# Moving the S5 tables, their loads and their parameters: which engine, which queue, which step

## The chip, the core and the metric

The kernel runs on one core of a Trainium2 chip (TensorE, VectorE, ScalarE, GpSimd and SyncE, with 16 DMA engines). The metric is the time of one execution in microseconds (us) on the device; less is better. In the profile the engines are PE, DVE, ACT, POOL and SP; TensorE's weight loads are PEld.

## What is computed

One layer of a hybrid encoder on 2048 tokens of 1024 channels, in float32. Cut to what matters here:

```python
h = rms_norm(x, norm_gain)
proj = einsum('bsd,de->bse', h, w_in)
q, k, v, z_attn, u_ssm, z_ssm, g = split(proj, SPLITS)          # 512,128,128,512,512,512,2048
attn = windowed_gqa(q, k, v, attn_sink, rel_bias_table) * silu(z_attn)
y = gelu(s5_bidirectional(u_ssm, a_re, a_im, log_dt, b_re, b_im, c_re, c_im, ssm_d))
y = y * sigmoid(y @ w_glu + b_glu)
ssm = y * silu(z_ssm)
merged = sigmoid(g_attn) * (attn @ w_branch_attn) + sigmoid(g_ssm) * (ssm @ w_branch_ssm)
return rms_norm(x + merged @ w_out, final_norm_gain)

def s5_bidirectional(u, ...):        # 32 groups of 16 channels, 64 states per group and direction
    for d in range(2):
        dt = exp(log_dt[d]);  a_bar = exp(lam * dt);  b_bar = b * (a_bar - 1) / lam
        x[t] = a_bar * x[t-1] + b_bar @ u[t]      # d = 1 runs backwards
        y   += Re(c @ x)
    y += d_skip * u
```

## The kernel before, in words

Every matrix product is made with each operand split into a high and a low part, by three matmuls (`mm3`, L215 to L225: L219 high by high, L220 low of h, L221 low of w). A projection is one 128-column strip of `w_in` against one block of 512 tokens: 8 x 3 = 24 matmuls.

**Stage one** (to some 170 us) makes h for four blocks of 512 tokens (`make_h`, its transposes on TensorE at L274), projects u, k and v of each (strips u0 to u3, k, v in the list `wlist`, index i), stores u in channel order as uS, and stores the h of blocks 0 and 1 in DRAM as hS (`spill`). v is turned over by transposes at L388. The parameters of the SSM are loaded and computed in it as well (`ssm_params`, L432 to L659): DMA issues on SP first (L443 for a, L455 for c), then eleven transposes (L468, L476), then 288 small VectorE instructions (most of them L481) that make powers and products of the states' factors.

**Stage two** (to some 1140 us) projects q, z_attn, z_ssm and the gates, and beside it runs a chain of side work: the SSM, then attention. **Stage three** is the GLU, the branches, the output projection and the last norm.

What sets the order: the program is written out in one pass, and side work is a Python generator. `mm3` calls `turn` or `tick` four times in a projection; each gives every side generator credit of half its rate, and a generator goes on to its next `yield` for each unit of credit. So a "step" (the work between two yields) of the chain falls behind a fixed number of projection matmuls, and every engine takes its instructions in the order in which they were written. Weights are split a strip ahead: the high part on ScalarE (L162), the low part on GpSimd in four pieces (`low_part`, L154). Loads are issued on SP (`nc.sync`), stores on ScalarE (`A`).

The SSM (`ssm`) works in 8 frames of 4 groups. Tokens are cut into 256 pieces of 8 (M = 256, T = 8). A frame i has 18 steps:

- `inject` (four times): W times U on TensorE (L829), copied into X by ScalarE (L830, L831);
- for each half: `rotate` by the tables ec, es (L838, L839, L841 on VectorE), `scan` (L850), rotate back, `high_h` (L857 on ScalarE) and `low_h` (L862 on VectorE), which make the parts Hh, Hl of the states;
- `emit` for each half: M times U (L872) and ws times H on TensorE, copied to Y by ScalarE (L880).

Beside it the frame prepares what later frames need. `prep_w`, `prep_o` and `prep_e` are tables of products (helper `product`, L684 to L686: two products and their sum or difference, tiles wt, wo, ec and es), all three on GpSimd but for frame 0. `mats` transposes wt on TensorE (L767) into Wh, Wl (L770, L761). `zmat` flips the sign of wo on ScalarE (`sign_o`, L731, and ncc, L733), multiplies it by b on TensorE (L792, L799) into Z, and stores Z to DRAM as zS (L803); `load_m` reads it back as the band matrix Ml in four DMAs (L809), and `load_u` reads the next U in four (L744), all on SP. `split_o`, `split_m`, `split_u` make high and low parts (L719 on ScalarE, L720 on VectorE); `mirror_e` fills the other half of ec, es (L716 on ScalarE).

```python
            if i == 0:
                yield from zmat(0)
                load_m(0)
...
                prep_o(nx)
...
            if nx:
                load_m(nx)
            if nn:
                load_u(nn, 0)
                load_u(nn, 1)
```

Of the kernel before, what the change touches and what calls it, by code (L numbers as in the profile page):

```python
# [21 lines left out]
NBLK = 4  # L22
COL_Q, COL_K, COL_V, COL_ZA, COL_U, COL_ZS, COL_G = 0, 512, 640, 768, 1280, 1792, 2304
G, P, C, T = 32, 64, 16, 8
M = S // T
GB = 4
RATE1 = 1.336
RATE2 = 1.237
RATE3 = 1.499
# [7 lines left out]
def kernel(  # L37
# [9 lines left out]
    nc = tc.nc  # L47
# [3 lines left out]
    out = out[0]  # L51
# [379 lines left out]
    eye = prm.tile([128, C], F32, name="eye")  # L431

    def ssm_params(pool):
        n_ = [0]
# [11 lines left out]
        for d in range(2):  # L446
            V.tensor_copy(raw[:, 2, d * 64:(d + 1) * 64], dt2[:, d:d + 1].to_broadcast([32, 64]))
        for src, dst in ((ssm_b_re, bb_re), (ssm_b_im, bb_im)):
# [20 lines left out]
        re, im, ld = sm(), sm(), sm()  # L469
        V.tensor_copy(re, pt[:, 0:32])  # L470
        V.tensor_copy(im, pt[:, 32:64])
        V.tensor_copy(ld, pt[:, 64:96])
        for i, dst in enumerate((cc_re, cc_im)):
# [4 lines left out]
        yield 1.5  # L478

        def tt(o, a, b, op):  # L480
            V.tensor_tensor(o, a, b, op)  # L481
            return o
# [44 lines left out]
        xi = tt(sm(), im, dt_, ALU.mult)  # L527
        yield 4
        sc, e1 = exp_parts(xr)
        ex = stt(sm(), e1, 1.0, sc, ALU.add, ALU.mult)  # L530
        em1 = tt(sm(), e1, sc, ALU.mult)
        stt(em1, sc, -1.0, em1, ALU.add, ALU.add)
        yield 4
        k = rnd(xi, 0.3183098861837907)
# [18 lines left out]
        cs = ts(sm(), cm, 1.0, None, ALU.add, None)  # L553
        yield 5
        ar = tt(pw_re[:, :, 1], ex, cs, ALU.mult)
# [33 lines left out]
        for i in range(2, T + 1):  # L589
            cmul(pw_re[:, :, i], pw_im[:, :, i], pw(i // 2), pw(i - i // 2))  # L590
        yield 8
        f, b_ = slice(0, 64), slice(64, 128)
        for dst_i, dst_o, src in ((wi_re, wo_re, pw_re), (wi_im, wo_im, pw_im)):
# [3 lines left out]
            V.tensor_copy(dst_o[b_], src[b_, :, T:0:-1])  # L597
        yield 8
        tb = [pool.tile([128, G, C], F32, tag=f"tb{i}", name=f"tb{i}") for i in range(4)]
# [7 lines left out]
        tt(bb_im, tb[2], tb[3], ALU.add)  # L607
        yield 4
        e8 = ts(sm(), xr, 8.0, None, ALU.mult, None)
# [42 lines left out]
        powers(el_re, el_im, 16)  # L652
        yield 4
        cmul(*hi(1), lo(8), lo(8))
        powers(eh_re, eh_im, 8)
        unit(el_re, el_im, 16)
        unit(eh_re, eh_im, 8)
        yield 4


    def ssm(pool):
# [10 lines left out]
        def product(o, p, q, eng):  # L672

            for n, (a, b, c, d, op) in enumerate(
                ((p[0], q[0], p[1], q[1], ALU.subtract), (p[0], q[1], p[1], q[0], ALU.add))
            ):
                for g in range(0, o[n].shape[1], 2):
                    gs = slice(g, g + 2)
                    if eng is Q:
                        tmp = [pool.tile([128, 2, T, C], F32, tag=f"t{m}", name=f"t{m}") for m in range(2)]  # L680
                    else:
                        r = rtile().rearrange("p g r m -> p (g r m)")
                        tmp = [r[:, m * 256:m * 256 + 256].rearrange("p (g j c) -> p g j c", g=2, c=C) for m in range(2)]
                    eng.tensor_tensor(tmp[0], a[:, gs], b[:, gs], ALU.mult)  # L684
                    eng.tensor_tensor(tmp[1], c[:, gs], d[:, gs], ALU.mult)  # L685
                    eng.tensor_tensor(o[n][:, gs], tmp[0], tmp[1], op)  # L686
# [53 lines left out]
        def load_u(i, half):  # L740
            lo = pool.tile([128, 2, M], F32R, tag=f"U{half}l", name=f"U{half}l", bufs=2)
            raw = lo.bitcast(F32)
            for j in range(2):
                nc.sync.dma_start(out=raw[:, j], in_=chan(uS, i * GB + half * 2 + j))  # L744
            raw_u[i, half] = lo, raw
# [29 lines left out]
        def zmat(i):  # L775

            g0 = i * GB
            s = st[i]
            sign_o(i)
            yield  # L780
            wo = raw_o[i]
            Z = pool.tile([128, 15 * C], F32, tag="Z", name="Z")
            pf, pb = bank("s2"), bank("s2")

            def two(t, g):

                return t[:, g0 + g:g0 + g + 2].rearrange("p g c -> p (g c)")

            for d, pt, o0, c0 in ((f, pf, 16, 0), (b_, pb, 0, 16)):
                for n, bt in enumerate((bx_re, bx_im)):  # L790
                    for g in range(GB):
                        PE.matmul(  # L792
                            pt[g * 32:(g + 1) * 32, o0:o0 + 112], two(bt, g)[d],
                            wo[n][:, g].rearrange("p j c -> p (j c)")[d, c0:c0 + 112], start=n == 0, stop=n == 1,
                        )
                yield
            for n, (bt, ct) in enumerate(((bx_re, cc_re[:, g0:g0 + GB]), (bx_im, s["ncc"]))):
                for g in range(GB):
                    PE.matmul(pf[g * 32:(g + 1) * 32, 0:16], two(bt, g), ct[:, g], start=n == 0, stop=n == 1)  # L799
            V.tensor_copy(Z[:, 0:112], pb[:, 0:112])  # L800
            V.tensor_copy(Z[:, 112:240], pf[:, 0:128])
            V.scalar_tensor_tensor(Z[:, 112:128], eye, dd[:, i:i + 1], Z[:, 112:128], ALU.mult, ALU.add)
            nc.sync.dma_start(out=zS[i], in_=Z)  # L803

        def load_m(i):
            lo = pool.tile([128, GB, 128], F32R, tag="Ml", name="Ml")
            raw = lo.bitcast(F32)
            for g in range(GB):
                nc.sync.dma_start(  # L809
                    out=raw[:, g],  # L810
                    in_=bass.AP(
                        tensor=zS.tensor, offset=zS.offset + (i * 128 + g * 32) * 15 * C,
                        ap=[[C, T], [15 * C, C], [1, 128]],
                    ),
                )
            st[i]["m"] = (lo, raw)
# [66 lines left out]

        def frame(i):

            nx = i + 1 if i + 1 < NB else None
            nn = i + 2 if i + 2 < NB else None
            ms = mats(nx) if nx else None
            zs = zmat(nx) if nx else None
            inject(i, 0)  # L890
            yield
            inject(i, 1)
            yield
            rotate(i, 0, 0)
            inject(i, 2)
            yield
            scan(i, 0)
            inject(i, 3)
            yield
            if i == 0:  # L900
                yield from zmat(0)
                load_m(0)
            rotate(i, 0, 1)
            if nx:
                next(ms)
                prep_e(nx, 0)
            yield
            split_o(i)
            if nx:
                next(ms)  # L910
                prep_o(nx)
            yield
            high_h(i, 0)
            rotate(i, 1, 0)
            if nx:
                next(ms, None)
            if nn:
                prep_w(nn)
            yield
            low_h(i)  # L920
            scan(i, 1)
            yield
            split_m(i)
            rotate(i, 1, 1)
            if nx:
                prep_e(nx, 1)
            yield
            yield
            yield from emit(i, 0)
            yield  # L930
            high_h(i, 1)
            if nx:
                mirror_e(nx, 0)
                next(zs)
            yield
            low_h(i)
            if nx:
                split_u(nx, 0)
                next(zs)
            yield  # L940
            if nx:
                split_u(nx, 1)
                mirror_e(nx, 1)
                next(zs)
            yield
            yield from emit(i, 1)
            if nx:
                next(zs, None)
            yield
            if nx:  # L950
                load_m(nx)
            if nn:
                load_u(nn, 0)
                load_u(nn, 1)
            st.pop(i)
            yield

        raw_o, ph = {}, {}
        load_u(0, 0)
        load_u(0, 1)  # L960
        prep_w(0, V)
        prep_e(0, 0)
        prep_e(0, 1)
        prep_o(0, V)
        for _ in range(3):
            yield
        split_u(0, 0)
        split_u(0, 1)
        yield from mats(0)
        mirror_e(0, 0)  # L970
        mirror_e(0, 1)
        load_u(1, 0)
        load_u(1, 1)
        prep_w(1)
        for i in range(NB):
            yield from frame(i)

# [238 lines left out]
    with tc.manual_schedule():  # L1216
# [85 lines left out]
        for b in range(NBLK):  # L1302
            gen = None
            for i, key in enumerate(wlist):
# [4 lines left out]
                if i == 1 and b + 1 < NBLK:  # L1309
                    gen = add_side(make_h(xp, b + 1), RATE1)  # L1310
                    if b + 2 < NBLK:
                        load_x(xp, b + 2)
                if b == 2 and i == 3:
                    s2.close()
                    spool = s1.enter_context(tc.tile_pool(name="spool", bufs=1))
                    bias_vectors(spool)
                    params = ssm_params(spool)
                    next(params)
                if b == 1 and i == 0:
                    load_bg2()  # L1320
                if b == NBLK - 1 and i == 0:
                    pr = add_side(params, 1.0)
                if b == NBLK - 1 and i == 2:
# [392 lines left out]
```

## Time and profile before

| | |
|---|---|
| median of 3 runs | 1615.24 us (1614.47 to 1616.01) |
| the profiled execution, its own time | 1614.77 us |
| its span, first to last instruction | 1612.7 us |
| busy: TensorE, VectorE, ScalarE, GpSimd | 1433.5, 1007.9, 654.9, 692.4 us |
| mean granted clock of TensorE | 0.948 of full speed |

The span is the time between the first and the last instruction in the trace; the time of an execution includes some 2 us around it. Busy shares are means over stages with different limits, so the stages are looked at by windows. A clock of 1.0 is 2.4 GHz, 0.5 is 1.2 GHz. A row of waits gives the waiting engine and line, what ended the wait, then the us in total, the number of waits and the longest.

### The profile page before, as it was taken

What the parts mean: (1) busy time and instruction counts of PE and PEld (TensorE: products, weight loads), DVE (VectorE), ACT (ScalarE), POOL (GpSimd) and SP (SyncE); (2) the same over time, 40 slices, a digit from 0 to 9 for tenths busy, and PEclk for the clock granted to TensorE, in tenths of its full rate; (3) what the DMA queues carried; (4) which work ended last, traced back from release to release, by engine and by line L of the source; (5) the groups of instructions that cost most, each with busy time, mean ns of one, the idle gap of its engine ahead of it and who ended that gap; (6) DMA issues with size and microseconds to landing.
All of it is one profiled execution on the core that took longest, in us unless ns stands there. A gap on an engine that the chain in (4) does not pass through costs nothing.

```text
span 1612.7 us, 19812 instructions
## 1 busy us (share of the span) xinstructions
PE 1433.5 (89%) x6933; PEld 1168.7 (72%) x6933; DVE 1007.9 (62%) x1940; ACT 654.9 (41%) x1197; POOL 692.4 (43%) x767
## 2 busy tenths in 40 slices
PE   7999486967969679788999999999988999998998
PEld 6787365756758567577888878888766787786886
DVE  3326966648475373862799999993468557376342
ACT  6332032423434234352566666663545234143211
POOL 5510159477695766872311111211249235053230
PEclk9999788978979789898999999999999999999999
DMA  7453021311313223244533333334577456375351
GB/s 251 149 121 86 18 97 46 101 62 66 108 48 104 69 67 108 72 134 131 150 89 91 94 93 92 92 92 131 157 195 210 156 143 168 127 187 173 111 144 65
DMA packets 240723, 185.48 MB, mean 115 GB/s; under 512 B 57920, under 2 KB 202432, under 8 KB 240624
## 3 DMA queue, kind: packets, MB, share of 16 engines
q10 hardware_dynamic: 108336, 100.61, 21.6%
q1 hardware_dynamic: 132288, 83.62, 17.4%
q8 instruction: 54, 0.88, 0.2%
q14 instruction: 45, 0.37, 0.1%
HBM read 126.56 MB, written 57.62 MB: 114 GB/s over the span
## 4 chain that ended last, share of the span: by engine, by line
PE 42%; POOL 14%; DVE 13%; DMA 6%; issue 6%; ACT 4%; ACTq 1%; SPq 0%; POOLq 0%; DVEq 0%
PE pj L221 8%; PE pj L219 8%; PE pj L220 8%; POOL t L684 4%; POOL t L685 4%; PE s L1562 3%; PE s L1563 3%; PE s L1564 3%; POOL wl L154 3%; PE s L1117 2%; PE s L1080 2%; PE s L1133 2%; DMA yt<-yS 2%; POOL wo L686 2%; POOL wt L686 1%
## 5 line engine op out<-in xcount | busy, mean ns | idle before, releaser
L154 POOL TENSOR_TENSOR wl<-raw,wh 128x256 fp32r<-128x256 f32 x380 | 340.9, 929 | 597.3 <-ACT wh L162 553.3
L221 PE MATMUL pj<-hh,wl 128*128 128x512 f32 x976 | 392.9, 403 | 34.9 <-POOL wl L154 34.8
L219 PE MATMUL pj<-hh,wh 128*128 128x512 f32 x976 | 396.6, 406 | 2.9 <-ACT wh L162 2.9
L220 PE MATMUL pj<-hl,wh 128*128 128x512 f32 x976 | 390.2, 400 | 0.0
L221 PEld LDWEIGHTS pj<-hh,wl 128*128 128x128 f32 x976 | 189.0, 194 | 80.5 <-POOL wl L154 38.2
L219 PEld LDWEIGHTS pj<-hh,wh 128*128 128x128 f32 x976 | 189.7, 194 | 41.7 <-issue 3.9
L220 PEld LDWEIGHTS pj<-hl,wh 128*128 128x128 f32 x976 | 189.8, 194 | 35.4
L162 ACT ACTIVATE wh<-raw 128x1024 fp32r<-128x1024 f32 x96 | 100.8, 1052 | 22.3 <-DMA raw<-in_w_glu_dram 5.1
L1562 PE MATMUL s<-woh,mh 128*128 128x512 f32 x256 | 102.4, 400 | 6.3 <-DVE xr L1569 6.3
L1563 PE MATMUL s<-wol,mh 128*128 128x512 f32 x256 | 102.0, 398 | 0.0
L1564 PE MATMUL s<-woh,ml 128*128 128x512 f32 x256 | 101.9, 398 | 0.0
L1120 ACT ACTIVATE ph<-s 128x512 fp32r<-128x512 f32 x92 | 54.5, 593 | 82.0 <-PE s L1117 80.0
L1606 POOL TENSOR_TENSOR sm<-sm,mhalf 128x1 f32<-128x1 f32 x15 | 8.3, 553 | 171.3 <-DVE sm L1605 134.7
L403 ACT ACTIVATE st<-pj,bg 128x512 f32<-128x512 f32 x64 | 43.9, 686 | 89.9 <-PE pj L221 83.9
L838 DVE TENSOR_TENSOR rt<-X,es 128x1020 f32<-128x1020 f32 x32 | 44.2, 1380 | 56.1 <-ACT X L831 50.5
L1097 ACT ACTIVATE p<-p,sml 128x384 f32<-128x384 f32 (+1 forms) x128 | 75.7, 594 | 6.7 <-DVE sml L1093 6.5
L1081 DVE CUSTOM_DVE_ANT_0 p<-s,bias 128x384 f32<-128x384 f32 (+1 forms) x128 | 68.5, 535 | 7.5 <-PE s L1080 6.2
L1122 DVE TENSOR_TENSOR pl<-s,ph 128x512 fp32r<-128x512 f32 x92 | 63.4, 689 | 13.2 <-ACT ph L1120 12.1
L1080 PE MATMUL s<-kst,qs 128*128 128x384 f32 (+1 forms) x256 | 65.9, 338 | 0.0
L1569 DVE TENSOR_TENSOR xr<-xr,s 128x512 f32<-128x512 f32 x32 | 21.9, 684 | 68.9 <-PE s L1564 68.9
L872 PE MATMUL s<-U0h,Ml 128*128 128x256 f32 x16 | 7.2, 447 | 64.9 <-DVE Ml L720 64.9
L862 DVE TENSOR_TENSOR Hl<-X,Hh 64x1024 fp32r<-64x1024 f32 x32 | 47.6, 1488 | 26.8 <-ACT Hh L857 26.5
(318 smaller groups left out, 3123.7 us busy)
## 6 DMA issues: line engine op xcount, KB each, us to landing
raw<-in_w_in_dram SPq DMA_DIRECT2D x59, 512.0 KB
gS<-st ACTq DMA_DIRECT2D x64, 256.0 KB
gt<-gS ACTq DMA_DIRECT2D x64, 256.0 KB
x<-in_x_dram SPq DMA_DIRECT2D x16, 512.0 KB
raw<-in_w_branch_attn_dram SPq DMA_DIRECT2D x32, 256.0 KB
raw<-in_w_branch_ssm_dram SPq DMA_DIRECT2D x32, 256.0 KB
out_dram<-xr ACTq DMA_DIRECT2D x15, 512.0 KB
xr<-in_x_dram SPq DMA_DIRECT2D x12, 512.0 KB
```

What stands on the lines that cost most here:

```text
L154: eng.tensor_tensor(lo[:, ks], r[:, ks], hi[:, ks].bitcast(F32), ALU.subtract)
L162: A.activation(res[0], r, AF.Copy)
L219: PE.matmul(pt, w[0][:, k], r[0][:, k], start=start and k == 0, stop=False)
L220: PE.matmul(pt, w[0][:, k], r[1][:, k], start=False, stop=False)
L221: PE.matmul(pt, w[1][:, k], r[0][:, k], start=False, stop=stop and k == kt - 1)
L684: eng.tensor_tensor(tmp[0], a[:, gs], b[:, gs], ALU.mult)
L1080: PE.matmul(pt[:, 0:w], s["qs"][:, h], kst[:, r, kv, k0 * 128:k1 * 128], start=r == 0, stop=r == 1)
L1081: V.tensor_tensor_reduce(out=p[:, h, 0:w], in0=pt[:, 0:w], in1=bias[:, kv * 4 + h, r0:r1:-1], scale=1.0, scalar=0.0, op0=ALU.add, op1=ALU. ...
L1097: A.activation(p[:, h, 0:w], p[:, h, 0:w], AF.Exp, bias=nm[:, j:j + 1], accum_out=den[:, j:j + 1])
L1562: PE.matmul(pt, mh[k][:, ts_], wo[0, n][:, k], start=k == 0, stop=False)
L1563: PE.matmul(pt, mh[k][:, ts_], wo[1, n][:, k], start=False, stop=False)
L1564: PE.matmul(pt, ml[k][:, ts_], wo[0, n][:, k], start=False, stop=k == KD - 1)
```

## The change

- Parameters: the DMA issues stand at block 2, strip 1 (before: strip 3); the transposes and the arithmetic follow from block 2, strip 2 at a rate of 2.2 steps (before: block 3, strip 0, rate 1.0). A recorder, `Later`, collects the 288 VectorE instructions, which are then issued six to a step in place of eight unequal parts.
- `prep_o` goes to VectorE, and `product` there works on whole tables (six instructions of 128x512 in place of twelve of 128x256).
- `load_u`, `load_m` and the store of Z are issued by ScalarE.
- The frame: 20 steps, in another order. zmat(i) begins at the end of frame i-1 and its last two parts stand in the first two steps of frame i; the store of Z is in the third, `load_m` two steps behind it; `split_m` comes right behind `split_o` and ahead of `low_h`; `low_h` comes ahead of the second half's rotation. What stands ahead of frame 0 is made to match.

The core of the diff (the removed yields between the parameters' parts, and the old frame, are left out; the old frame is in the listing above):

```diff
+RATEP = 2.2
...
+    class Later:
+        def __init__(self):
+            self.ops = []
+        def __getattr__(self, name):
+            return lambda *a, **k: self.ops.append(lambda: getattr(nc.vector, name)(*a, **k))
...
+        V = Later()
...
-        yield 4
-
+        for n, op in enumerate(V.ops):
+            op()
+            if n % 6 == 5:
+                yield
...
-                for g in range(0, o[n].shape[1], 2):
+                for g in range(0, o[n].shape[1], 2 if eng is Q else GB):
                     if eng is Q:
+                        gs = slice(g, g + 2)
...
                     else:
-                        r = rtile().rearrange("p g r m -> p (g r m)")
-                        tmp = [r[:, m * 256:m * 256 + 256].rearrange("p (g j c) -> p g j c", g=2, c=C) for m in range(2)]
+                        gs = slice(0, GB)
+                        r = rtile().rearrange("p g r m -> p g (r m)")
+                        tmp = [r[:, m].rearrange("p (g j c) -> p g j c", g=GB, c=C) for m in range(2)]
...
-                nc.sync.dma_start(out=raw[:, j], in_=chan(uS, i * GB + half * 2 + j))
+                A.dma_start(out=raw[:, j], in_=chan(uS, i * GB + half * 2 + j))
...
-            nc.sync.dma_start(out=zS[i], in_=Z)
+            s["z"] = Z
...
-                nc.sync.dma_start(
+                A.dma_start(
                     out=raw[:, g],
...
+        def frame(i, zs):
             ms = mats(nx) if nx else None
             inject(i, 0)
+            next(zs)
             yield
             inject(i, 1)
+            next(zs, None)
             yield
             rotate(i, 0, 0)
+            A.dma_start(out=zS[i], in_=st[i].pop("z"))
             inject(i, 2)
             yield
             scan(i, 0)
             inject(i, 3)
             yield
             rotate(i, 0, 1)
+            load_m(i)
             if nx:
                 next(ms)
+            yield
+            if nx:
                 prep_e(nx, 0)
+                next(ms)
+            yield
+            if nx:
+                next(ms, None)
+            if nn:
+                prep_w(nn)
+            split_o(i)
+            yield
+            split_m(i)
+            high_h(i, 0)
             yield
             low_h(i)
+            rotate(i, 1, 0)
+            yield
             scan(i, 1)
             yield
             rotate(i, 1, 1)
             if nx:
                 prep_e(nx, 1)
             yield
             yield from emit(i, 0)
             yield
             high_h(i, 1)
+            yield
+            low_h(i)
             if nx:
                 mirror_e(nx, 0)
+            yield
             if nx:
+                prep_o(nx, V)
                 split_u(nx, 0)
+            yield
+            yield from emit(i, 1)
             if nx:
                 split_u(nx, 1)
                 mirror_e(nx, 1)
+                if nn:
+                    load_u(nn, 0)
+                    load_u(nn, 1)
+                zn = zmat(nx)
+                next(zn)
+                yield
+                next(zn)
+                nz.append(zn)
+                yield
             st.pop(i)
...
-                if b == 2 and i == 3:
+                if b == 2 and i == 1:
                     s2.close()
...
                     params = ssm_params(spool)
                     next(params)
+                if b == 2 and i == 2:
+                    pr = add_side(params, RATEP)
...
-            if b == NBLK - 1 and i == 0:
-                pr = add_side(params, 1.0)
```

Where instructions stand, before and in the change (a number behind an x counts like instructions in a row; lines of the change are some 10 later than those of before from `product` on).

TensorE in stage one, around the parameters' eleven transposes (sm is a parameter's tile, st the v to be turned over, x the input tile of `make_h`). Before:

```order
L388 MATMUL s_911<-ident,st 128x128 x4
...
L221 MATMUL pj<-hh,wl 128x512
L274 MATMUL s_1008<-ident,x 128x128 x4
...
L468 MATMUL s_1193<-ident,sm_1026 128x32 x3
L476 MATMUL s_1203<-ident,sm_1039 128x128 x4
```

In the change:

```order
L389 MATMUL s_911<-ident,st 128x128 x4
...
L222 MATMUL pj<-hh,wl 128x512
L478 MATMUL s_1023<-ident,sm_944 128x32 x3
L486 MATMUL s_1033<-ident,sm_957 128x128 x4
L486 MATMUL s_1039<-ident,sm_960 128x128 x4
...
L275 MATMUL s_1129<-ident,x 128x128 x4
```

The parameters' transposes moved from behind the transposes of the last block's x to ahead of them, 42 projection matmuls behind the turning of v.

ScalarE at the end of a frame (Y is emit's result, U1h a high part of U, ec and es the mirrors, wo the sign flip, th, zaS and zsS belong to projections). Before:

```order
L880 ACTIVATE Y<-s_2842 128x512
L93 DMA zaS<-st 128x512
L857 ACTIVATE Hh<-X 64x1024 x2
L716 ACTIVATE ec<-ec 128x2x127
L716 ACTIVATE es<-es 128x2x127
L731 ACTIVATE wo_2694<-wo_2694 128x512
L733 ACTIVATE ncc<-cc_im 128x64
L399 ACTIVATE th<-pj 128x512
```

In the change:

```order
L888 ACTIVATE Y<-s_2905 128x512
L727 ACTIVATE U1h<-U1l 128x512
L724 ACTIVATE ec<-ec 128x2x127
L724 ACTIVATE es<-es 128x2x127
L752 DMA U0l<-uS 128x1x256 x2
L752 DMA U1l<-uS 128x1x256 x2
L739 ACTIVATE wo_2880<-wo_2880 128x512
L741 ACTIVATE ncc<-cc_im 128x64
L94 DMA zsS<-st 128x512
L400 ACTIVATE th<-pj 128x512
```

The sign flip moved from ahead of the second emit's Y to behind it and behind the four loads of U, which ScalarE now issues.

VectorE between the low parts of H and the scans (Wl, ws, Ml and U are low parts, X the states, rt a scratch tile). Before:

```order
L761 TENSOR_TENSOR Wl<-s_2686,Wh 128x512
L862 TENSOR_TENSOR Hl<-X,Hh 64x1024 x2
L850 SCALAR_TENSOR_TENSOR X<-rho,X 128x255 x4
L720 TENSOR_TENSOR Ml<-Ml,Mh 128x512
L838 TENSOR_TENSOR rt<-X,es 128x4x255
```

In the change, the same place of a frame, and the end of that frame:

```order
L728 TENSOR_TENSOR Ml<-Ml,Mh 128x512
L870 TENSOR_TENSOR Hl<-X,Hh 64x1024 x2
L846 TENSOR_TENSOR rt<-X,es 128x4x255
...
L870 TENSOR_TENSOR Hl<-X,Hh 64x1024 x2
L692 TENSOR_TENSOR rt<-wo_re,cc_re 128x512
L693 TENSOR_TENSOR rt<-wo_im,cc_im 128x512
L694 TENSOR_TENSOR wo_2879<-rt 128x512
L692 TENSOR_TENSOR rt<-wo_re,cc_im 128x512
L693 TENSOR_TENSOR rt<-wo_im,cc_re 128x512
L694 TENSOR_TENSOR wo_2880<-rt 128x512
L728 TENSOR_TENSOR U0l<-U0l,U0h 128x512
```

The low part of M moved from behind the scans of the second half to ahead of the low parts of H, and the table wo joins VectorE's queue between the second low parts and U.

## Rows read from the trace of the kernel before

**Rows 1.** The page: busy us, share and instructions of each engine, and TensorE's granted clock in 40 slices of the span (tenths).

```profile
PE 1433.5 (89%) x6933; PEld 1168.7 (72%) x6933; DVE 1007.9 (62%) x1940; ACT 654.9 (41%) x1197; POOL 692.4 (43%) x767
PEclk9999788978979789898999999999999999999999
```

**Rows 2.** Windows: a stretch in us and its length, busy us (and instructions) of PE, PEld, DVE, ACT and POOL, the granted clock, the DMA engines' share and GB/s.

```profile
160.00:760.00 600.00, 470.14 (x2473) 384.33 (x2472) 373.31 (x546) 205.40 (x318) 388.38 (x408) 0.87 0.26 81
760.00:1140.00 380.00, 374.09 (x1876) 314.81 (x1876) 311.29 (x900) 229.86 (x556) 73.96 (x88) 1.00 0.36 105
```

**Rows 3.** Waits of TensorE from 160 to 770 us: tile and line that waited, what ended the wait, us in total, times, longest.

```profile
PE s L872 <- DVE Ml L720: 64.9, 8, 10.5
PE pj L221 <- POOL wl L154: 34.8, 6, 8.5
PE s L767 <- issue: 22.7, 1, 22.7
PE s L829 <- DVE U0l L720: 4.1, 1, 4.1
PE s L767 <- DVE wt L686: 1.7, 1, 1.7
PE s L829 <- DVE Wl L761: 1.0, 1, 1.0
```

**Rows 4.** Windows over the 15 stretches between 179 and 736 us in which the granted clock was 0.5: their sum, and the mean of one.

```profile
sum 153.70, PE 73.03 PEld 59.82 DVE 115.64 ACT 12.04 POOL 124.04; mean PE 4.87 PEld 3.99 DVE 7.71 ACT 0.80 POOL 8.27
```

**Rows 5.** Timeline of TensorE: start, length, what; in brackets the idle time before it.

```profile
98.83 0.60 PE L388 MATMUL s<-ident,st 128*128 128x128 f32 x4
...
112.92 0.60 PE L274 MATMUL s<-ident,x 128*128 128x128 f32 x4
...
199.55 0.66 PE L767 MATMUL s<-ident,wt 128*128 128x128 f32 x2 [22.71 <-issue]
```

**Rows 6.** Waits of SP's queue over the whole span.

```profile
SPq L744 <- DVE eh_im L481: 45.1, 1, 45.1
SPq L443 <- DMA hS<-hx: 43.9, 1, 43.9
...
SPq L809 <- DMA zS<-Z: 20.9, 8, 3.7
```

**Rows 7.** Timeline of SP's queue: start and length of the issue, and what is loaded or stored.

```profile
105.12 0.33 SPq L443 DMA_DIRECT2D sm<-in_ssm_a_re_dram  x1
...
115.55 1.05 SPq L455 DMA_DIRECT2D sm<-in_ssm_c_im_dram  x2
...
197.48 1.35 SPq L744 DMA_DIRECT2D U0l<-uS  x2
198.88 1.20 SPq L744 DMA_DIRECT2D U1l<-uS  x2
...
238.40 0.35 SPq L803 DMA_DIRECT2D zS<-Z  x1
241.61 2.48 SPq L809 DMA_DIRECT2D Ml<-zS  x4
```

**Rows 8.** Timeline of VectorE: the first parameter instruction, a product of the parameters, and the first two instructions of the first table.

```profile
135.05 0.19 DVE L470 COPY sm<-s 128x32 f32<-128x32 f32 x1 [2.98 <-PE s L468]
...
168.47 0.68 DVE L481 TENSOR_TENSOR tb<-bx_im,sm 128x512 f32<-128x512 f32 x1
...
197.51 0.43 DVE L684 TENSOR_TENSOR rt<-wi_re,bx_re 128x256 f32<-128x256 f32 x1
197.85 0.84 DVE L685 TENSOR_TENSOR rt<-wi_im,bx_im 128x256 f32<-128x256 f32 x1
```

**Rows 9.** VectorE's groups from 160 to 770 us, shapes apart: out<-in, shape, count | busy us, mean ns of one | idle before.

```profile
L841 DVE TENSOR_TENSOR X<-X,rt 128x510 f32<-128x510 f32 x64 | 61.7, 1004 | 1.1
L850 DVE TENSOR_TENSOR_SCAN X<-rho,X 128x255 f32<-128x255 f32 x64 | 56.9, 948 | 0.1
L862 DVE TENSOR_TENSOR Hl<-X,Hh 64x1024 fp32r<-64x1024 f32 x32 | 47.6, 1488 | 26.8 <-ACT Hh L857 26.5
L839 DVE TENSOR_TENSOR X<-X,ec 128x1020 f32<-128x1020 f32 x32 | 47.0, 1468 | 1.1
L838 DVE TENSOR_TENSOR rt<-X,es 128x1020 f32<-128x1020 f32 x32 | 44.2, 1380 | 56.1 <-ACT X L831 50.5 <-issue 5.4
...
L720 DVE TENSOR_TENSOR ws0l<-wo,ws0h 128x512 fp32r<-128x512 f32 x8 | 9.2, 1147 | 0.0
```

**Rows 10.** The same of GpSimd.

```profile
L154 POOL TENSOR_TENSOR wl<-raw,wh 128x256 fp32r<-128x256 f32 x116 | 105.6, 943 | 145.3 <-ACT wh L162 123.3 <-DMA U1l<-uS 12.3 <-DMA yS<-Y 9.6
...
L686 POOL TENSOR_TENSOR wo<-t,t 128x256 f32<-128x256 f32 x28 | 32.3, 1153 | 2.2
L686 POOL TENSOR_TENSOR wt<-t,t 128x256 f32<-128x256 f32 x28 | 25.2, 900 | 2.2
...
L686 POOL TENSOR_TENSOR ec<-t,t 128x256 f32<-128x256 f32 x16 | 15.6, 974 | 28.0 <-DVE X L839 27.1
```

**Rows 11.** The same of ScalarE.

```profile
L716 ACT ACTIVATE ec<-ec 128x254 f32<-128x254 f32 x16 | 6.6, 413 | 25.4 <-POOL ec L686 25.3
...
L719 ACT ACTIVATE U1h<-U1l 128x512 fp32r<-128x512 f32 x8 | 5.0, 624 | 2.0 <-DMA U1l<-uS 1.4 <-ACT st L403 0.6
...
L731 ACT ACTIVATE wo<-wo 128x512 f32<-128x512 f32 x8 | 4.9, 618 | 0.0
```

More of the change, by code (lines that the diff above doesn't have):

```diff
@@ L446, in ssm_params @@
         for d in range(2):
-            V.tensor_copy(raw[:, 2, d * 64:(d + 1) * 64], dt2[:, d:d + 1].to_broadcast([32, 64]))
+            nc.vector.tensor_copy(raw[:, 2, d * 64:(d + 1) * 64], dt2[:, d:d + 1].to_broadcast([32, 64]))
         for src, dst in ((ssm_b_re, bb_re), (ssm_b_im, bb_im)):
@@ L469, in ssm_params @@
         re, im, ld = sm(), sm(), sm()
-        V.tensor_copy(re, pt[:, 0:32])
-        V.tensor_copy(im, pt[:, 32:64])
-        V.tensor_copy(ld, pt[:, 64:96])
+        nc.vector.tensor_copy(re, pt[:, 0:32])
+        nc.vector.tensor_copy(im, pt[:, 32:64])
+        nc.vector.tensor_copy(ld, pt[:, 64:96])
         for i, dst in enumerate((cc_re, cc_im)):
@@ L532, in ssm_params @@
         stt(em1, sc, -1.0, em1, ALU.add, ALU.add)
-        yield 4
         k = rnd(xi, 0.3183098861837907)
@@ L553, in ssm_params @@
         cs = ts(sm(), cm, 1.0, None, ALU.add, None)
-        yield 5
         ar = tt(pw_re[:, :, 1], ex, cs, ALU.mult)
@@ L590, in ssm_params @@
             cmul(pw_re[:, :, i], pw_im[:, :, i], pw(i // 2), pw(i - i // 2))
-        yield 8
         f, b_ = slice(0, 64), slice(64, 128)
@@ L597, in ssm_params @@
             V.tensor_copy(dst_o[b_], src[b_, :, T:0:-1])
-        yield 8
         tb = [pool.tile([128, G, C], F32, tag=f"tb{i}", name=f"tb{i}") for i in range(4)]
@@ L607, in ssm_params @@
         tt(bb_im, tb[2], tb[3], ALU.add)
-        yield 4
         e8 = ts(sm(), xr, 8.0, None, ALU.mult, None)
@@ L652, in ssm_params @@
         powers(el_re, el_im, 16)
-        yield 4
         cmul(*hi(1), lo(8), lo(8))
@@ L882, in emit @@
                 store(chan(yS, i * GB + half * 2 + j), Y[:, j * M:(j + 1) * M])
-        def frame(i):
+        def frame(i, zs):
             nx = i + 1 if i + 1 < NB else None
@@ L888, in frame @@
             ms = mats(nx) if nx else None
-            zs = zmat(nx) if nx else None
             inject(i, 0)
+            next(zs)
             yield
             inject(i, 1)
+            next(zs, None)
             yield
             rotate(i, 0, 0)
+            A.dma_start(out=zS[i], in_=st[i].pop("z"))
             inject(i, 2)
@@ L899, in frame @@
             yield
-            if i == 0:
-                yield from zmat(0)
-                load_m(0)
             rotate(i, 0, 1)
+            load_m(i)
             if nx:
                 next(ms)
+            yield
+            if nx:
                 prep_e(nx, 0)
+                next(ms)
             yield
[L908 to L914, printed above, removed]
             if nx:
@@ L927, in frame @@
             yield
-            yield
             yield from emit(i, 0)
@@ L931, in frame @@
             high_h(i, 1)
-            if nx:
-                mirror_e(nx, 0)
-                next(zs)
             yield
@@ L937, in frame @@
             if nx:
+                mirror_e(nx, 0)
+            yield
+            if nx:
+                prep_o(nx, V)
                 split_u(nx, 0)
-                next(zs)
             yield
+            yield from emit(i, 1)
             if nx:
@@ L943, in frame @@
                 mirror_e(nx, 1)
[L944 to L954, printed above, removed]
+                if nn:
[7 more added lines that the diff above has]
+                yield
             st.pop(i)
-            yield
-        raw_o, ph = {}, {}
+        raw_o, ph, nz = {}, {}, []
         load_u(0, 0)
@@ L963, in ssm @@
         prep_e(0, 1)
+        yield
         prep_o(0, V)
-        for _ in range(3):
-            yield
+        yield
+        yield from mats(0)
         split_u(0, 0)
         split_u(0, 1)
-        yield from mats(0)
+        zn = zmat(0)
+        next(zn)
         mirror_e(0, 0)
         mirror_e(0, 1)
+        yield
+        next(zn)
+        nz.append(zn)
         load_u(1, 0)
@@ L974, in ssm @@
         prep_w(1)
+        yield
         for i in range(NB):
-            yield from frame(i)
+            yield from frame(i, nz.pop())
     def bias_vectors(pool):
```

3 lines of the change are left out of this document (removed).

## The prediction, made before the changed kernel ran

> **What bounds it now.** Start on the page: TensorE is busy 89% of the span, no other engine more than 62%, and the granted clock dips only between a tenth and a half of the span [rows 1]. So the time is TensorE's work plus its holes, and the holes lie in the stage with the SSM frames. The windows confirm it: from 160 to 760 us TensorE is busy 470 of 600 us at a mean clock of 0.87, while in the attention stretch behind it is busy 374 of 380 at full clock [rows 2]. That stretch and all behind it I leave alone: the change touches nothing there, and the order of their work is the same.
>
> TensorE's waits name the holes [rows 3]: 64.9 us before the first emit matmul (L872) for the split of M, 34.8 us for low parts of weights that GpSimd brings late (L221), 22.7 and 1.7 us at the first transposes of a W table (L767), 4.1 and 1.0 us at injections (L829): together 129.2 us. Idle time also costs clock: in the stage lie 15 stretches at the lower of the two levels (0.5, 1.2 GHz), in which TensorE was busy 73.0 us [rows 4]; at 2.4 GHz that work takes half, so 36.5 us are lost, 2.4 us a stretch. The profiled execution took 1614.8 us (0.5 below the median of the runs, 1615.2). Without any hole the stage would end 165.7 us sooner: **a floor of 1449**. The prediction is that floor plus the holes that the new order leaves or makes.
>
> **The change, part by part.**
>
> *Parameters.* In stage one they start a block earlier. The eleven parameter transposes now stand 42 projection matmuls behind the flip at 98.83 us [rows 5]; sixty matmuls lie between the end of that flip (some 99.2) and the transposes at 112.92 [rows 5], so one takes 0.229 us and TensorE is there at about 108.8. The loads do not come earlier: SP's queue stood 43.9 us waiting for a store of hS before it issued the first of them [rows 6], at 105.12, and the last load of c is issued until 116.6 [rows 7]. Neither the store nor its queue has moved. With 2.6 us for a transfer (SP waits 20.9 us in eight times for the round trip of Z, [rows 6]) the data are there at 119: **TensorE waits 9.8 us** where it waited for nothing. Bounds: 2.5, if the c loads issue as fast as the first ones, and 12. All of stage one's matmuls are queued behind it.
>
> The parameter work itself is 288 VectorE instructions. Before, it ran from 135.05 to about 197 [rows 8], and the first tables behind it gave the 22.7 us. Now it starts at 119 instead of 135; by its old length of 62 us it would end at 181, and I add 8 us since the last 30 instructions or so (products of 0.68 among them, [rows 8]) are issued only when the last projection of stage one is, one behind the other: 189. TensorE came to the first transposes at 176.8 (199.55 less 22.7, [rows 5]); they now stand 6 matmuls earlier (1.4 us) and behind the new wait: 185. So it waits 4 us for the parameters. The tables then take VectorE three to six instructions of 0.43 to 1.15 each [rows 8, 9]. I take **8 us** at the first tables and Z (bounds 3 and 14), against 24.4 now.
>
> *The Z chain.* L872 waits because Z is computed, stored, loaded and split within half a frame. In the new order Z's second half opens the next frame, its load stands two steps behind the store, and the split of M goes ahead of the low parts of H. A step of the frame is 186 / 20 = 9.3 projection matmuls of 0.229 us, 2.1 us; the split stands three steps behind the load (6.4 us) and emit(0) seven (15 us). The load's four issues (2.48 us, [rows 7]), its 2.6 us and the split (0.62 on ScalarE, 1.10 on VectorE) fit in. **L872's 64.9 us go.**
>
> What is late next is Z's front. Its matmuls read wo after the sign flip (L731) on ScalarE. In the new order that stands behind the copy of Y and the high part of U1 (0.62 each by the latter), two mirrors (2 × 0.41) and the four loads of U now issued by ScalarE, which took SP 1.35 + 1.20 [rows 7, 11]; then itself 0.62: 5.2 us behind emit(1). TensorE gets there after 6 matmuls (1.4 us) in three frames and 12 (2.7 us) in four: 3 × 3.8 + 4 × 2.5 = **21 us**. Bounds: 0 if ScalarE issues for nothing and Y is copied at once, 37 if all 5.2 lie on the path seven times. Behind the flip wait the conversions of the next projection and the injections' copies, so a delay here goes round the frame.
>
> *GpSimd.* prep_o leaves it: 84 instructions in seven tables, 97 us by the 1.15 us of their sums [rows 10]. GpSimd's late low parts have cost 34.8 us in six waits of 5.8. In three frames prep_w (12 instructions, 10.8 us by 0.90 each) still stands directly ahead of a weight's low parts (0.94 a quarter), and prep_e still waits for rotate-back to free its buffers (27.1 us by [rows 10]). I keep three waits of three quarters of 5.8: **13 us** (bounds 0 and 34.8).
>
> *VectorE.* prep_o comes to it as six instructions of 128x512 a frame. Such an instruction took 0.68 us in stage one [rows 8] and 1.15 among the frames [rows 9]; I take 1.10 as nearest in place: 6.6 us a frame, 46 in all. VectorE's frame is then four rotations of 4.86, eight scans of 0.95, four low_h of 1.49 [rows 9], about 9 of splits and copies (five at 1.15, four at 0.68, Z) and 6.6: 48.5 us. TensorE's frame, now 186 projection matmuls, is 42.6 us, plus sixty matmuls of half the width and 32 small ones, about 9: 51.6. VectorE just fits; for single links that come late I take **6 us** (bounds 0 and 39, see below). Here a rule weighs against the row. The row: one instruction among the frames costs 0.47 us more than alone.
>
> The Trainium skill, "SBUF — State Buffer", section "Who interferes with whom", says that a VectorE instruction with two SBUF inputs and a GpSimd one that reads SBUF exclude each other, the later waiting for the whole of the earlier. By it up to one GpSimd instruction (0.93 us) would be added to each of the 42, 39 us instead of 6, and the sum would be some 33 us higher. The trace agrees in direction (0.43 and 0.84 us for two like instructions in a row), not in that size.
>
> *Queues.* U, M and Z leave SP's queue, where the first U loads waited 45.1 us for the parameters [rows 6]; the injections' 4.1 and 1.0 go with them. ScalarE gains nine issues a frame: 0.35 + 2.48 + 2.55 = 5.4 us [rows 7]. It is busy 205 of 600 us [rows 2], so only the 2.55 counted above lie on the path. The load of Ml would hold ScalarE for 2.6 us if it came right behind the store; it comes two steps, 4.3 us, later.
>
> *Clock.* Three holes in front and about 6.5 in the frames at 2.4 us: **23 us**.
>
> Sum: 1449 + 9.8 + 8 + 21 + 13 + 6 + 23 = **1530**, 85 below the profiled execution, which stands as near the median as said. With every term half way to its bound at once (VectorE's upper one is left to its rival) the forecast's own range is 1504 to 1553.
>
> **Rivals.**
>
> *The cover holds.* ScalarE issues its loads while TensorE does something else, and VectorE's links come in time. For it: ScalarE is idle two thirds of the stage. Against it: the flip really stands behind the issues in the order. Only the front (10 + 8 and 7 of clock) and the weights' 13 with 2 of clock remain: 1449 + 25 + 13 + 2 = 1489.
>
> *VectorE becomes the frame's bound.* Its chain has 3 us of slack; if every new instruction is held by GpSimd for a whole instruction, a frame grows by 6 × 0.93 = 5.6 us, seven times 39, with 6 more of clock: 1575. For it: the doubled instruction in [rows 8]. Against it: GpSimd has 97 us less to do. The page named above would have it so.
>
> *ScalarE's queue holds the chain: slower.* Its nine issues a frame are 72 in all, and ScalarE keeps order: whatever waits in an issue holds X, H and every projection's eviction. It decides from (1614.8 − 1530) / 72 = 1.2 us on the path for each; at 2.6 us, a round trip of Z [rows 6], it adds 187 less what is hidden: 1640 to 1700. For it: SP did wait 20.9 us there. Against it: the load is two steps behind the store, and an issue took 0.3 to 0.7 us.
>
> That nothing moves would need new holes to equal old ones by chance.
>
> **Numbers.** Forecast 0.60; cover holds 0.17; VectorE bounds 0.18; slower 0.04; the same 0.01 (within 0.2%, 3.2 us, about what a measurement of this kernel can tell). Faster by more than that: 0.95. The range takes the forecast and most of the two cases at its sides, each with its own few us about it: 1483 to 1582.
>
> **What would show it.** In the new profile: a TensorE wait of about 10 us at the parameter transposes near 109 us; L872's waits gone; instead waits at Z's first matmuls released by ScalarE's wo; L221's waits at about 13 us; a frame of some 57 us; VectorE's table instructions at 1.1 us, GpSimd down by 97 us. It is wrong if emit still waits for M, if TensorE's largest waits are for VectorE's rotations or scans (second rival), if ScalarE's issues last over a microsecond (third), or if the attention stretch is no longer full.

## The result, and the profile after

The changed kernel takes 1531.58 us (median of 4 runs, 1529.46 to 1531.99) against 1615.1 before: ratio 0.948, 95% interval 0.9463 to 0.9496. The prediction was 1530 in a range of 1483 to 1582.

The page of the changed kernel, its busy times and clock, to be held against [rows 1]:

```profile
PE 1421.8 (93%) x6933; PEld 1155.5 (76%) x6933; DVE 1038.0 (68%) x1970; ACT 655.8 (43%) x1197; POOL 641.2 (42%) x683
PEclk9999999999999989999999999999999999999999
```

GpSimd has 84 instructions fewer, but only 51 us less work; VectorE has 30 us more. TensorE's waits from 90 to 690 us (the stage with the frames now ends some 70 us earlier), which answer to [rows 3]; lines from `product` on are 8 higher, L800 is Z's first matmuls, L739 the sign flip, L775 the first transposes of W, L486 those of the parameters c:

```profile
PE pj L222 <- POOL wl L155: 33.0, 6, 7.4
PE s L800 <- ACT wo L739: 16.8, 7, 8.1
PE s L486 <- DMA sm<-in_ssm_c_re_dram: 8.1, 1, 8.1
PE s L775 <- issue: 4.0, 1, 4.0
PE s L389 <- ACT st L384: 0.7, 1, 0.7
```

Together 62.6 us against 129.2. Windows over the ten stretches at the lower clock between 113 and 636 us, which answer to [rows 4]:

```profile
sum 61.40, PE 42.46 PEld 33.61 DVE 41.62 ACT 22.59 POOL 47.45; mean PE 4.25 PEld 3.36 DVE 4.16 ACT 2.26 POOL 4.75
```

Half of 42.46, 21.2 us, is lost to the clock, by its two levels (in these stretches a matmul of 512 columns comes every 0.43 us, at the higher level every 0.23, so it is a little less). Floor, waits and clock make 1449 + 62.6 + 21.2 = 1532.8; the profiled execution took 1529.5. The attention stretch is as full as before (366.9 of 370 us, [rows 2] had 374.1 of 380). So the account closes within 3.3 us, and the gain is what the waits and the clock say.

### The profile page after: what moved, and what is told of

It reads as the page before. It is cut to its first block, busy times and chain, and to the rows that moved or that the text cites. A ratio compares the mean times of both kernels' runs of the same rounds, so it can differ in the third digit from the quotient of the medians.

```text
span 1527.7 us, 19701 instructions
## 1 busy us (share of the span) xinstructions
PE 1421.8 (93%) x6933; PEld 1155.5 (76%) x6933; DVE 1038.0 (68%) x1970; ACT 655.8 (43%) x1197; POOL 641.2 (42%) x683
## 3 DMA queue, kind: packets, MB, share of 16 engines
q1 hardware_dynamic: 122432, 76.34, 16.8%
## 4 chain that ended last, share of the span: by engine, by line
PE 43%; DVE 14%; POOL 13%; DMA 6%; issue 6%; ACT 5%; ACTq 1%; POOLq 0%; SPq 0%; DVEq 0%
PE pj L220 8%; PE pj L222 8%; PE pj L221 8%; POOL wl L155 3%; PE s L1574 3%; POOL t L692 3%; PE s L1575 3%; PE s L1576 3%; POOL t L693 3%; DMA yt<-yS 3%; PE s L1145 2%; PE s L1092 2%; PE s L1129 2%; POOL wt L694 2%; DVE X L847 1%
## 5 line engine op out<-in xcount | busy, mean ns | idle before, releaser
L155 POOL TENSOR_TENSOR wl<-raw,wh 128x256 fp32r<-128x256 f32 x380 | 348.8, 949 | 598.4 <-ACT wh L163 584.1
L221 PEld LDWEIGHTS pj<-hl,wh 128*128 128x128 f32 x976 | 187.6, 192 | 34.8
L1109 ACT ACTIVATE p<-p,sml 128x384 f32<-128x384 f32 (+1 forms) x128 | 75.8, 595 | 16.8 <-DVE sml L1105 16.8
L1581 DVE TENSOR_TENSOR xr<-xr,s 128x512 f32<-128x512 f32 x32 | 21.9, 685 | 69.2 <-PE s L1576 69.2
L849 DVE TENSOR_TENSOR X<-X,rt 128x510 f32<-128x510 f32 x64 | 62.4, 1015 | 1.1
L1574 PEld LDWEIGHTS s<-woh,mh 128*128 128x128 f32 x256 | 48.4, 189 | 18.8 <-DVE xr L1581 7.2
L1092 PE MATMUL s<-kst,qs 128*128 128x384 f32 (+1 forms) x256 | 61.7, 342 | 0.6 <-issue 0.6
L1614 ACT ACTIVATE jk<-xr 128x1024 bf16<-128x1024 f32 x15 | 15.9, 1057 | 97.7 <-DVE xr L1581 97.7
```

The costliest lines, as they stand in the source:

```text
L155: eng.tensor_tensor(lo[:, ks], r[:, ks], hi[:, ks].bitcast(F32), ALU.subtract)
L221: PE.matmul(pt, w[0][:, k], r[1][:, k], start=False, stop=False)
L1092: PE.matmul(pt[:, 0:w], s["qs"][:, h], kst[:, r, kv, k0 * 128:k1 * 128], start=r == 0, stop=r == 1)
L1109: A.activation(p[:, h, 0:w], p[:, h, 0:w], AF.Exp, bias=nm[:, j:j + 1], accum_out=den[:, j:j + 1])
L1574: PE.matmul(pt, mh[k][:, ts_], wo[0, n][:, k], start=k == 0, stop=False)
```

## The experiments

Each was timed against the kernel before on the same chip (1613 to 1615 us), and a ratio is to that time. A difference in us between two runs can be off by some 2 us where their chips differ.

**a1: the split of M alone, in the kernel before.**

```diff
+            split_m(i)
             low_h(i)
             scan(i, 1)
             yield
-            split_m(i)
             rotate(i, 1, 1)
```

> The kernel before with one line moved: the split of M stands ahead of the low parts of H instead of behind the scans of the second half. Order theory: emit waited for M (64.9 us) only because its low part stood behind 3.3 us of low_h and 4.0 us of scans in VectorE's queue; now low_h comes 1 us later and emit waits some 2.5 us for it, eight times 20 us, so waits fall by 45 and clock gives back some 12: about 1558. Queue theory (M's data come late because SP's queue is held by weight loads): no change, 1615. VectorE theory (its whole chain is late, whatever stands first): the wait only changes its name to Hl, above 1600.

1612.22 us, ratio 0.999 (0.9977 to 1.0002): no change, so the figure of the order theory fell. Its waits (L876 is ws times H, L792 Z's first matmuls):

```profile
PE pj L221 <- POOL wl L154: 57.4, 9, 13.3
PE s L767 <- issue: 22.7, 1, 22.7
PE s L876 <- DVE Hl L862: 18.6, 8, 2.7
PE s L792 <- ACT wo L731: 10.1, 2, 6.4
PE s L872 <- DVE Ml L720: 9.0, 5, 3.0
```

The mechanism is there as expected: M's 64.9 us became 9.0, and Hl took 18.6 in its place. But TensorE then only met the next late thing: the weights' low parts from GpSimd went from 34.8 to 57.4 us and the flip of wo (a table made by GpSimd then) from nothing to 10.1. The other two theories had the time right, but not the reason. M's data were there, since an earlier split took 55.9 us off the wait for it; and the wait did not simply change its name to Hl, which took 18.6 of them.

**c1: prep_o on VectorE alone, in the kernel before.**

```diff
-                prep_o(nx)
+                prep_o(nx, V)        # and product in whole tables for VectorE
```

> The kernel before with one thing alone: the table wo on VectorE in six instructions, at its old place. If either limit alone holds the old frame (M's split late in VectorE's queue, or GpSimd's late low parts), taking 97 us from GpSimd gives back little by itself: the waits for weights fall from 34.8 to under 10, and emit's for M grow from 64.9 to 100 or more, since 6.6 us more stand ahead of the split; 1600 to 1640. If GpSimd alone was the limit: 1560 to 1575.

1609.37 us, ratio 0.9971 (0.996 to 0.9983). The mirror image of a1 (its lines are one higher than in the kernel before):

```profile
PE s L873 <- DVE Ml L721: 104.3, 8, 16.5
PE s L768 <- issue: 23.5, 1, 23.5
PE s L793 <- ACT wo L732: 2.9, 2, 1.9
```

No wait for weights is left, and M's grew by 39 us, six instructions more standing ahead of its split. So this run relieves GpSimd and burdens VectorE's order at once.

**a3: the new order, with prep_o back on GpSimd.**

```diff
-            if nn:
-                prep_w(nn)
             split_o(i)
+            if nx:
+                prep_o(nx)
             yield
+            if nn:
+                prep_w(nn)
...
-                prep_o(nx, V)
```

> The changed kernel with the table wo made by GpSimd again (12 instructions a frame, where it stood before: behind the split of wo; the W table a step behind it). GpSimd theory: GpSimd is then busy 57 us of a frame of 59, late low parts of weights wait twice as long as now (33 to over 60 us) and the tables come late: 1570 to 1590. Rival: since the late low parts cost 34.8 us before and 33.0 in the changed kernel, 97 us less work on GpSimd bought nothing: 1528 to 1540.

1585.36 us, ratio 0.9817 (0.98 to 0.9833): as the GpSimd theory said.

```profile
PE pj L222 <- POOL wl L155: 87.5, 7, 16.3
PE s L800 <- ACT ncc L741: 9.1, 1, 9.1
...
PE s L800 <- ACT wo L739: 5.4, 6, 1.6
```

The three runs belong together. VectorE's order and GpSimd's load each held the old frame: taking away one gave 0.1 to 0.3%, while in the new order prep_o on VectorE is worth 54 us (1585.4 to 1531.6). Two things stay open. In a3 the W table also stands a step later than in the change, so the 54 us are of the move and of the tables' places together. And a1 and c1 were not run together in the old frame, so no run tells how much the rest of the new order (Z's earlier front, `low_h` ahead of the rotation, two steps more) adds to those two edits.

**a4: the parameters where they were.** The loads at block 2, strip 3, transposes and arithmetic from block 3, strip 0, in the old eight parts:

```diff
-                if b == 2 and i == 1:
+                if b == 2 and i == 3:
...
-                if b == 2 and i == 2:
-                    pr = add_side(params, RATEP)
+                if b == NBLK - 1 and i == 0:
+                    pr = add_side(params, 1.0)
```

> The changed kernel with the parameters' loads, transposes and instructions where they stood before. Front theory: the wait of 8.1 us for the c loads goes, the first tables' 4.0 us become some 24, and the clock loses 2 to 8 more: 1540 to 1552. Rival: what the front loses is made up by later waits of the first frame: 1528 to 1536.

1539.49 us, ratio 0.9538 (0.9523 to 0.9554), at the lower edge of the front theory. The first transposes of W wait 24.8 us, the parameters' not at all; the waits for weights and for the flip are as in the changed kernel to 0.6 us. The earlier parameters are worth 8 us, of the 83.

**b3: the parameters' transposes two projections later than in the change.**

```diff
-RATEP = 2.2
+RATEP = 2.9
...
-                if b == 2 and i == 2:
+                if b == 2 and i == 4:
```

> The changed kernel with the parameters' transposes two projections (48 matmuls) later, and 2.9 steps instead of 2.2 for each unit of credit, so that they end as early. If the wait of 8.1 us for c is paid for nothing: it goes, with 2 us of clock, 1520 to 1525. If the parameters then end later by what they start later: the first tables' wait grows from 4.0 to 10 or more and the time stays at 1528 to 1533.

1535.1 us, ratio 0.9511 (0.9494 to 0.9529): no gain, and 2 us past the upper end of the second case. The wait for c went, and the first transposes of W waited 14.3 us instead of 4.0. What the parameters' chain starts later it ends later.

**a2: U, M and Z on SP's queue.** All three `A.dma_start` of the change back to `nc.sync.dma_start`.

> The changed kernel with the loads of U and M and the store of Z issued by SP again. Order theory: the queue is worth nothing by itself, 1526 to 1540. Queue theory: SP stands waiting for weight buffers, Z's store and M's load come late, and emit waits for M again: over 1560, with waits at emit's first matmul of 5 us or more in most frames.

1523.6 us, ratio 0.9439 (0.9425 to 0.9453): *faster* by 8 us, a little beyond the order theory's edge. No emit waits for M, so the queue theory falls for the new order too, and the move to ScalarE cost time: the waits for the flip are 10.2 us here, 16.8 in the change.

```profile
PE s L800 <- ACT wo L739: 10.2, 5, 7.9
```

**b1: the flip ahead of the second emit.**

```diff
+            if nx:
+                zn = zmat(nx)
+                next(zn)
             yield from emit(i, 1)
...
-                zn = zmat(nx)
-                next(zn)
```

> The changed kernel with the sign flip of wo ahead of the second emit, so ahead of the copy of Y, the high part of U1, the mirrors and the four loads of U on ScalarE. If those four stand in the way of Z's matmuls: their waits for the flip fall from 16.8 to under 9 us (the one long wait, behind loads of h, may stay), 1521 to 1527. If the flip then waits for VectorE's table wo and holds Y and the loads: 1530 to 1536.

1519.47 us, ratio 0.9414 (0.9394 to 0.9435): 12 us faster, 1.5 beyond the first case. One wait for the flip is left, 3.7 us:

```profile
PE s L800 <- ACT wo L739: 3.7, 1, 3.7
```

**b2: the W table in four parts.**

```diff
-                prep_w(nn)
+            next(pw4, None)      # in four steps: with high_h(0), ahead of emit(0),
+                                 # with high_h(1), ahead of prep_o; three instructions each
```

> The changed kernel with the W table in four parts of three GpSimd instructions, in four steps of the frame instead of one; the work is the same. Order theory of GpSimd (low parts of weights are late because up to 18 table instructions stand in one piece ahead of them): the waits for them fall from 33.0 us to 5 to 12, with 4 to 8 us of clock: 1497 to 1508. Amount theory (GpSimd has too much to do in a frame, wherever it stands): the waits move to other weights, 1526 to 1534.

1528.05 us, ratio 0.9465 (0.9445 to 0.9486), which can't be told from the change (its interval overlaps): the time that the amount theory gave. Yet the weights came (lines here and in d2 and d4 are 11 higher than in the change: L811 is Z's first matmuls, L895 ws times H):

```profile
PE s L811 <- ACT wo L750: 25.8, 7, 7.7
...
PE s L895 <- DVE Hl L881: 6.7, 4, 3.8
PE pj L222 <- POOL wl L155: 6.4, 3, 2.8
```

33.0 us became 6.4, as the order theory of GpSimd said of the waits; the flip took 9 us of it, Hl and Hh (3.6) 10. ScalarE's timeline behind one emit of this kernel (ACTq is its queue of issues):

```profile
500.04 0.41 ACT L735 ACTIVATE ec<-ec 128x254 f32<-128x254 f32 x1
500.33 0.58 ACTq L763 DMA_DIRECT2D U1l<-uS  x1
500.34 0.40 ACT L735 ACTIVATE es<-es 128x254 f32<-128x254 f32 x1
506.32 0.58 ACTq L763 DMA_DIRECT2D U1l<-uS  x1
506.95 0.63 ACT L750 ACTIVATE wo<-wo 128x512 f32<-128x512 f32 x1 [6.21 <-DMA raw<-in_w_in_dram]
```

The fourth load of U is issued 5.4 us after the third was done, and the flip stands behind it; a frame later it is 5.0 us. At these two places the waits for the flip are 6.9 and 5.2 us, 1.6 and 2.8 in the change. That is the third rival of the prediction, in small: ScalarE held in an issue.

**d1, d2, d3, d4: what these point to.** d1 is the change with the edits of a2 and b1; d2 is d1 with that of b2; d3 is d1 with the loads of c ahead of b's:

```diff
-        for src, dst in ((ssm_b_re, bb_re), (ssm_b_im, bb_im)):      # the loads of b,
+        # ... now behind the loop over ssm_c_re, ssm_c_im
```

d4 has all four.

> The changed kernel with U, M and Z on SP's queue and the flip ahead of the second emit (the two edits that each were faster alone, 1523.6 and 1519.5). If both took away the same wait (Z's matmuls behind ScalarE's queue): 1516 to 1521. If SP's queue gives something beyond it: 1509 to 1515.

1517.64 us, ratio 0.9408 (0.9378 to 0.9439): not to be told from b1, so the two edits took the same wait.

> The kernel d1 with the W table in four parts. If those parts gave only 3.5 us alone because Z's matmuls then waited behind ScalarE's queue (16.8 to 25.8 us), they now give most of the 26 us of weight waits: 1496 to 1506. If VectorE's chain is the next limit (waits for Hl, Hh and for wo from VectorE): 1510 to 1518, with those waits at 15 us or more.

1496.27 us, ratio 0.9272 (0.9238 to 0.9306). The same edit that gave nothing measurable in b2 gives 21 us here, where ScalarE's queue is out of the way; Hl and Hh (3.5) keep 10 us.

```profile
PE pj L222 <- POOL wl L155: 6.3, 3, 2.8
PE s L811 <- ACT wo L750: 4.4, 2, 3.7
```

> The kernel d1 with the parameter loads of c ahead of those of b on SP's queue; b's took SP 4.6 us. If the parameters' whole chain hangs on c, the wait at their transposes falls from 8.2 to some 3.5 us and the first tables do not come later: 5 to 8 us less than d1. If the first tables wait longer by what is gained, no change.

1509.26 us, ratio 0.935 (0.9325 to 0.9376): 8.4 us less than d1, just past the first case. The wait at the transposes of c fell to 2.2 us, and the first tables wait as before (4.3).

> All four edits together: U, M and Z on SP, the flip ahead of the second emit, the W table in four parts, the loads of c ahead of those of b. If the c loads act on stage one alone, they take the same 8.4 us from d2 (1496.3) as from d1: 1485 to 1491. If VectorE's chain at the front of the frames takes them back: 1493 to 1498.

**1486.67 us** (5 runs, 1486.24 to 1491.32), ratio 0.9225 (0.9212 to 0.9238): 45 us faster than the change (41 by the two ratios). What is left in its waits:

```profile
PE s L895 <- DVE Hl L881: 6.7, 4, 3.8
PE pj L222 <- POOL wl L155: 6.3, 3, 2.8
PE s L786 <- issue: 4.3, 1, 4.3
PE s L811 <- ACT wo L750: 4.2, 2, 3.7
PE s L895 <- ACT Hh L876: 3.5, 2, 1.9
```

## Why the prediction was right, and where it was not

The time was right to 1.6 us, and that closely by luck, for errors cancelled: weights +20, against tables −4, Z's front −4, VectorE −6, parameters −2 and clock −2.

- *The floor* (1449) holds, as the account above shows.
- *L872's 64.9 us go:* right, none is left. That they would come off the time rested on the other engines keeping up, which the sum counted but the prediction did not say: a1 shows that moving the split alone gives nothing.
- *The parameters' new wait:* 9.8 forecast (its own 119 less 108.8 would be 10.2), 8.1 measured, at 109 us, for c, as said:

```profile
108.64 0.39 PE L478 MATMUL s<-ident,sm 32*128 32x32 f32 x3
...
117.14 1.09 PE L486 MATMUL s<-ident,sm 128*128 128x128 f32 x4 [8.11 <-DMA sm<-in_ssm_c_re_dram]
```

- *The first tables:* 8 forecast, 4.0 measured (within 3 to 14).
- *Z's front:* 21 forecast, 16.8 measured; the place and releaser are right, the make-up is not. I set 5.2 us of ScalarE's work behind emit in one line. One frame's end:

```profile
257.96 0.60 ACT L888 ACTIVATE Y<-s 128x512 f32<-128x512 f32 x1 [4.28 <-PE s L884]
258.01 0.63 ACTq L752 DMA_DIRECT2D U0l<-uS  x1
258.46 0.63 ACT L727 ACTIVATE U1h<-U1l 128x512 fp32r<-128x512 f32 x1
258.68 0.60 ACTq L752 DMA_DIRECT2D U0l<-uS  x1
258.98 0.41 ACT L724 ACTIVATE ec<-ec 128x254 f32<-128x254 f32 x1
259.28 0.41 ACT L724 ACTIVATE es<-es 128x254 f32<-128x254 f32 x1
259.31 1.20 ACTq L752 DMA_DIRECT2D U1l<-uS  x2
260.56 0.63 ACT L739 ACTIVATE wo<-wo 128x512 f32<-128x512 f32 x1 [0.87 <-issue]
```

The issues run beside the activations; the flip starts 2.6 us behind the start of Y's copy, not 4.6, and 0.87 us of it is the issues'. So five waits are 1.6 us or less, and in one of them (0.9, at 320 us) the flip itself had waited 1.55 us for the table wo, which VectorE makes now. The other two (2.8 and 8.1) have other causes: the fourth load of U held 2.6 us in its issue, and ScalarE waiting 9.8 and 1.7 us for h from DRAM:

```profile
623.79 1.06 ACT L1245 ACTIVATE hh<-raw 128x1024 fp32r<-128x1024 f32 x1 [9.77 <-DMA raw<-hS]
...
628.52 1.06 ACT L1245 ACTIVATE hh<-raw 128x1024 fp32r<-128x1024 f32 x1 [1.68 <-DMA raw<-hS]
...
631.09 0.62 ACT L739 ACTIVATE wo<-wo 128x512 f32<-128x512 f32 x1
```

- *GpSimd,* the step that failed: "I keep three waits of three quarters of 5.8: 13 us"; it was six of 5.5, 33.0. Two assumptions were wrong. I left GpSimd's instructions at their old lengths, and with VectorE busier they grew (below): W's sums from 0.90 to 1.20 us, those of ec from 0.97 to 1.25, the low parts from 0.94 to 1.07, which is why 97 us left it and the page shows 51. And up to 18 table instructions still stand in one piece ahead of a weight, while TensorE comes sooner: b2 shows it by spreading them, which takes away 26.6 of the 33.0 us. How much of the 33.0 the longer instructions cost no run tells apart.
- *VectorE:* its new instructions cost 1.04 to 1.15 us (1.10 forecast), and it held TensorE up once, by the 0.9 us above (6 forecast). d2 shows it as next: 6.7 us of Hl, and 3.5 of Hh, which ScalarE makes from VectorE's X.
- *Queues:* costed at nothing beyond the 2.55 us in Z's front. By a2, ScalarE's issues cost 8 us in all; the waits show 6.6 of it at the flip.
- *Clock:* 9.5 stretches at 2.4 us forecast; ten at 2.1 measured.
- *The frame:* 57 us forecast, 62.3 measured (from 231.8 to 667.7 us in seven frames, by emit's first matmul, L880; 69.2 before). Of the 5.3 us too many, 2.9 are the weights' (their 20 us over seven frames).

Of the rivals, "cover holds" failed on the weights, and on Z's front, where it had no wait; VectorE did not become the bound. The third rival was real in one frame, with the 2.6 us of the fourth load.

## What to carry over

A wait's size in a trace is not what its removal brings: the engine then stands at the next late thing, and two limits can each look worthless to remove when tried alone (a1, c1, and b2 against d2). Work out every engine's frame, and when work moves between GpSimd and VectorE, lengthen the other instructions of both. Keep short conversions on which TensorE waits ahead of DMA issues in an engine's order, and spread side work over steps rather than put it in one piece ahead of work that is due.

## What the runs showed of the hardware

GpSimd's two-input instructions depend on what VectorE does beside them. The same kind of instructions of the W table, in the kernel before while VectorE had next to nothing to do (one instruction of 0.69 us):

```profile
334.96 0.62 POOL L684 TENSOR_TENSOR t<-wi_re,bx_re 128x256 f32<-128x256 f32 x1
335.54 0.62 POOL L685 TENSOR_TENSOR t<-wi_im,bx_im 128x256 f32<-128x256 f32 x1
336.25 0.74 POOL L686 TENSOR_TENSOR wt<-t,t 128x256 f32<-128x256 f32 x1
```

and in the changed kernel, beside a rotation of VectorE (its L846 runs from 411.94 for 1.53 us, L847 from 413.50 for 1.52):

```profile
410.90 1.49 POOL L692 TENSOR_TENSOR t<-wi_re,bx_re 128x256 f32<-128x256 f32 x1
412.35 1.59 POOL L693 TENSOR_TENSOR t<-wi_im,bx_im 128x256 f32<-128x256 f32 x1
414.02 1.60 POOL L694 TENSOR_TENSOR wt<-t,t 128x256 f32<-128x256 f32 x1
```

These three end at 412.39, 413.94 and 415.62, each some half a microsecond behind the end of an instruction of VectorE (411.91, 413.47 and 415.02). c1, in which only prep_o moved, shows the mean: W's sums went from 0.90 to 1.15 us. In the changed kernel they took 1.20, and in a3, its order with prep_o still on GpSimd, 1.03:

```profile
L687 POOL TENSOR_TENSOR wt<-t,t 128x256 f32<-128x256 f32 x28 | 32.2, 1149 | 2.2
...
L694 POOL TENSOR_TENSOR wt<-t,t 128x256 f32<-128x256 f32 x28 | 33.6, 1200 | 2.2
...
L694 POOL TENSOR_TENSOR wt<-t,t 128x256 f32<-128x256 f32 x28 | 28.8, 1029 | 2.2
```

The Trainium skill, "SBUF — State Buffer", section "Who interferes with whom", says that such instructions of the two engines exclude each other and that the later one waits for the whole of the earlier. The timelines agree, in that GpSimd's 0.62 to 0.74 us became 1.49 to 1.60, ending behind VectorE's. In the prediction I let it lengthen VectorE's side alone, but GpSimd's paid as well. That a port is what they share no run here shows by itself.

An issue of a DMA can hold ScalarE for microseconds (5.4 us from one load of U to the next in b2, 2.6 in the change), where most took 0.6. What held it (the trace names a weight's load) was not tried apart.
